# Attention scores: two products of 128 rows each in place of one of 128 and one of 64 rows

## The chip, the cores and the metric

The kernel runs on one core of a Trainium2 chip. The metric is the device time of one execution in microseconds (us), the median of several runs. The engines are written as in the profile: PE is the matrix engine (PEld its weight load, PEq its sequencer), DVE the vector engine, ACT the scalar engine, POOL GpSimd, SP the engine that issues the transfers (SPq is its queue).

## The reference

One layer of a decoder trunk on 256 tokens of width 1024, in float32. Only the two attention branches matter here:

```
h = rms_norm(x, norm_mix_g);  proj = h @ w_in
qa, ka, va, qc, kc, vc, rx, rgate, gates = split(proj)
# branch a: 8 heads of 64; one block of 256 keys, so causal attention with ALiBi
l = einsum('bhqd,bhkd->bhqk', q, k) * 64**-0.5 - slopes * dist     # -inf where dist < 0
ya = softmax(l) @ v
# branch c: 4 heads, two maps of 64 each
p = softmax(same logits);  w = p[map 0] - lam * p[map 1];  yc = rms_norm(w @ v) ...
# branch b: a linear recurrence.  Then gates, output projection, and a gated MLP with a convolution
```

There are 8 score maps in branch a and 8 in branch c, each of 256 queries by 256 keys with a depth of 64.

## The kernel before

**Arithmetic.** Every factor of a product is split into two float32r parts, a high part (the value rounded by ACT) and a low part (the exact rest, by DVE); a product is the sum of hi·hi, hi·lo and lo·hi. `mm3` (lines 110 to 112) issues these three for the projections, with 256 tokens as moving columns.

**Weight stream.** The weights come in 77 chunks of [128, 2048], 1 MB each, in the order of their use. SP loads a chunk into one of three `raw` buffers (line 86). ACT and DVE split each half of a chunk into `whi` and `wlo` (lines 96 and 97), four halves ahead of PE. Chunks 4 and 5 are q of branch a, 6 and 7 its k, 8 and 9 its v (`va`), 10 to 15 q, k and v of branch c, then gates and branch projections. Half n is the first or second half of chunk n // 2.

**Side work.** Attention, convolution and recurrence are side work of the main stream: the table `SL` names the chunk beside which each piece is written, and a scheduler that also places instructions by its own estimate puts them into each engine's order. Each engine, SP's queue included, works through its order from front to back.

**Scores.** q and k of a branch lie as 4 tiles of 128 rows, two heads of 64 in each. `stack_q` and `stack_k` copy them by transfers from SBUF to SBUF (line 395, 64 rows, 256 KB each) into `QS`, which holds q hi in rows 0 to 63 and q lo in rows 64 to 127 of each of 8 maps, and `KS`, which holds k hi twice. `att_scores` computes a map (tile `a0s` to `a7s`, `c00s` to `c31s`) in two halves of 128 queries, j = 0 and 1, into one PSUM bank. For each, line 458 multiplies QS by KS over 128 rows, (q hi + q lo)·k hi, and line 459 adds q hi·k lo over the 64 rows in which that head lies. Both have 256 keys as columns. DVE then adds the ALiBi distances and takes the row minimum (line 464; of j = 0 it reads 128 keys only), and ACT takes the exponential (line 467).

**Buffers.** Large tiles share SBUF by tags: a tile of a tag waits until the readers of the tile before it are done. `q0` holds `qka` (q hi and k lo of branch a) and later `mg`, the sum of the gated branches; `s10` holds `ocs`, the outputs of branch c.

Of the kernel before, what the change touches and what calls it, by code (L numbers as in the profile page):

```python
# [13 lines left out]
P = 128  # L14
S = 256
# [14 lines left out]

# where the side work goes: the first chunk beside which it is done, and over how many it is spread
SL = dict(norm=(4, 2.0), conv=(18, 5.5), moba=(8, 7.0), lag_a=(3, 5), diff=(16, 3.33), lag_c=(2, 4),
          gate=(19, 4.5), rga=(24, 5.0), rgb=(26, 4.0), rgc=32, rgd=(32, 1.5), rgy=(33, 1.5), df=22, sqa=6, ska=7,
          sqc=14, skc=13, lrgw=16, raw_up=20, h2=16, x1t=5)

# the weights in the order of their use, in chunks of [128, 2048]
ORDER = [(_n, _i) for _n, _c in (("rx", 4), ("qa", 2), ("ka", 2), ("va", 2), ("qc", 2), ("kc", 2), ("vc", 2),
# [10 lines left out]

# columns of the packed per-channel parameters
PC = {}  # L50
# [9 lines left out]
def hybrid_trunk(ctx: ExitStack, tc: tile.TileContext, x, wts, par, rgw, lqk, gf, out):  # L60
# [16 lines left out]

# [1 line left out]
    raws, his, los = {}, {}, {}  # L79
# [9 lines left out]
    def split_to(n):  # L89
        """Halves of chunks, up to the n-th, into a float32r part and the exact rest."""  # L90
        while state["split"] < min(n, 2 * NCHUNK):
            i = state["split"]
            raw = raws[i // 2][:, (i % 2) * HC:(i % 2 + 1) * HC]
            his[i] = wsp.tile([P, HC], F32R, name=f"whi{i}", tag="whi")
            los[i] = wsp.tile([P, HC], F32R, name=f"wlo{i}", tag="wlo")
            A.activation(his[i], raw, AF.Copy)  # L96
            V.tensor_tensor(los[i], raw, his[i].bitcast(F32), ALU.subtract)  # L97
            state["split"] += 1
# [14 lines left out]

# [1 line left out]
    # the first norm's gain comes with x, in the 8 columns before it  # L115
    xg_in = big.tile([P, KD * S + KD], F32, name="xg_in", tag="s0")
# [24 lines left out]

# [1 line left out]
    ones = const.tile([P, P], F32, name="ones")  # L143
# [8 lines left out]
    dist = const.tile([P, S], F32, name="dist")  # L152
    # the first q's are scaled by -1/(8 slope), a power of two, head by head
    qsc = const.tile([P, 4], F32, name="qsc")
    for h in range(8):
        G.memset(qsc[64 * (h % 2):64 * (h % 2) + 64, h // 2:h // 2 + 1], -0.125 * 2.0 ** (h + 1))

# [1 line left out]
    xgh = big.tile([P, KD, S], F32R, name="xgh", tag="s1")  # L159
# [15 lines left out]
    def rstd_of(ss_ap, n, scale, name):  # L175
        """1/sqrt(ss*scale + eps), from a table value and one Newton step."""
        m = work.tile([P, n], F32, name=name + "m", tag="nt_m", bufs=1)
        y = work.tile([P, n], F32, name=name + "y", tag="nt_y", bufs=1)
        t = work.tile([P, n], F32, name=name + "t", tag="nt_t", bufs=1)
        r = work.tile([P, n], F32, name=name + "r", tag="rstd", bufs=1)  # L180
        newton(y, m, t, r, ss_ap, scale)
        return r

    def sumsq_bcast(sq, k, src, name, later=False):
        """Adds tiles k, k+1 of src**2 up in sq; the last call sums over the partitions."""
        A.activation(sq[:, k:k + 2, :], src[:, k:k + 2, :], AF.Square)
        if k:
            (G if k < 6 else V).tensor_tensor(sq[:, 0:2, :], sq[:, 0:2, :], sq[:, k:k + 2, :], ALU.add)
        if k == 6 and not later:
            return sumsq_mm(sq, name)  # L190
# [5 lines left out]

# [1 line left out]
    # tiles 0..3, contraction outermost, so that each piece of x and of the weights is used as it lands  # L198
    rx_banks = [mm_bank(f"rxb{b}") for b in range(2)]
# [29 lines left out]
    def T_chunk(i, name, ah, al, evac, nk=KD, kouter=False):  # L229
        """Chunk of 128-wide output tiles; two tiles a bank; evac(bank, first tile)."""  # L230
        nt = HC // (nk * P)
# [37 lines left out]
    def norm_split(hf, hh, hl, src, gain, rstd, k):  # L269
        """Tiles k, k+1 of the normalised rows in two parts."""  # L270
        for j in (k, k + 1):
            V.scalar_tensor_tensor(hf[:, j, :], src[:, j, :], gain[:, j:j + 1], rstd, op0=ALU.mult, op1=ALU.mult)
        s = slice(k, k + 2)
        A.activation(hh[:, s, :], hf[:, s, :], AF.Copy)
        V.tensor_tensor(hl[:, s, :], hf[:, s, :], hh[:, s, :].bitcast(F32), ALU.subtract)
# [8 lines left out]

# [1 line left out]
    sm = const.tile([P, 12, 8], F32, name="sm")  # L286
# [12 lines left out]
    G.tensor_scalar(sm[:, 7], lam_c, -1.0, 0.0, op0=ALU.mult, op1=ALU.max)  # L299
    # sm[8] = softplus(-lambda); the gates are r = (tanh(.)+1)/2  # L300
    G.tensor_scalar(sm[:, 6], sm[:, 6], 2.0, None, op0=ALU.mult)
# [13 lines left out]

# [1 line left out]
    xr = big.tile([P, KD, S], F32, name="xr", tag="s6")  # L317
# [40 lines left out]
    def rg_b(s):  # L358
        """u = 1/(1+t2), refined from (1+exp)/2; a = (1-t2)*u;  -b = sqrt(t2)*(-u)*(2 i x)."""
        V.tensor_scalar(u0[:, s], u0[:, s], 0.5, 0.5, op0=ALU.mult, op1=ALU.add)  # L360
# [13 lines left out]

# [1 line left out]
    # q and k in two float32r parts; QS holds [q hi; q lo] and KS [k hi; k hi] of one map in its 128 rows, so that  # L376
    # one product gives (q hi + q lo) * k hi
    qk = big.tile([P, 8, S], F32R, name="qka", tag="q0")
# [3 lines left out]
    att = {}  # L382
    for n, tq, tk, t1, t2_ in (("a", None, None, "s0", "s9"), ("c", "q6", "q7", "s1", "s2")):
        att[n] = dict(
# [4 lines left out]
            QS=big.tile([P, 8, S], F32R, name="QS" + n, tag=t1),  # L389
            KS=big.tile([P, 8, S], F32R, name="KS" + n, tag=t2_))  # L390

    def stack(dst, row, src):
        """The heads of src's lower and upper rows, in turn, to 64 rows of dst."""
        for o in range(2):
            nc.sync.dma_start(dst[row:row + 64, o::2, :].bitcast(F32), src[64 * o:64 * o + 64, :, :].bitcast(F32))
# [35 lines left out]
    def stack_k(n):  # L431
        stack(att[n]["KS"], 0, att[n]["kh"])
        stack(att[n]["KS"], 64, att[n]["kh"])

    def v_chunks(i, name, dst):
# [15 lines left out]
    def att_scores(n, u, sl, st, name):  # L451
        """Probabilities of one map, unnormalised, with their reciprocal row sums."""
        t, o = u // 2, 64 * (u % 2)
        d = att[n]
        ps = at_bank(name + "s")
        for j in range(2):
            o_ = ps[:, j * S:(j + 1) * S]
            T.matmul(o_, lhsT=d["QS"][:, u, j * P:(j + 1) * P], rhs=d["KS"][:, u, :], start=True, stop=False)
            T.matmul(o_, lhsT=d["qh"][o:o + 64, t, j * P:(j + 1) * P], rhs=d["kl"][o:o + 64, t, :], start=False,
                     stop=True)  # L460
        mn = work.tile([P, 6], F32, name=name + "mn", tag="mn", bufs=8)
# [76 lines left out]
    def rg_y(s):  # L538
        """yb = h * gelu(gate); tr holds -h."""
        if s.start == 0:  # L540
# [7 lines left out]

# [1 line left out]
    sides = {}  # L550
# [16 lines left out]

    # slots are chunk positions: 4 qa, 6 ka, 8 va, 10 qc, 12 kc, 14 vc, 16 g0, 20 ba, 22 g2, 26 bc, 28 rg, 32 g1
    def slot(what, i, n):
# [98 lines left out]

# [1 line left out]
    x1 = big.tile([P, KD, S], F32, name="x1", tag="s6")  # L670
# [16 lines left out]

# [1 line left out]
    h2f = big.tile([P, KD, S], F32, name="h2f", tag="s7")  # L689
# [28 lines left out]

    # the down projection has the tokens in its rows, and so has all that follows
    x1T = big.tile([P, 2, D], F32, name="x1T", tag="s2")  # L720
# [14 lines left out]
    def finish(h, c):  # L735
        """Residual and norm of the columns c*512.. of 128 tokens."""
        o = slice(c * 512, (c + 1) * 512)
# [17 lines left out]
    for name, idx in FFN_ORDER:  # L755
# [13 lines left out]
        else:  # L769
# [4 lines left out]
            if idx == last - 1:  # L774
                # brings the table in before the end; the value is not used
                A.activation(sm[:, 11], acts[last][:, 1, 0, 0:8].bitcast(F32), AF.Abs_reciprocal_sqrt, bias=eps_s,
                             scale=0.0)
                pos += 1
                continue
            # the last two chunks: one half of the tokens after the other  # L780
            for h, c, i, e in ([(h, c, i, e) for h in range(2) for c in range(2) for i in (last - 1, last)
# [86 lines left out]
```

## Time and profile before

| | |
|---|---|
| Time, median of 3 runs | 501.83 us (503.34, 500.37, 501.83) |
| Span of the profiled execution, first to last instruction | 498.7 us |
| What lies between the median and that span | 3.1 us |
| PE busy | 488.2 us, 98% of the span |
| DVE, ACT busy | 383.3 and 306.6 us, 77% and 61% |
| Mean granted clock of PE | 0.986 |
| Moved by transfers | 90.50 MB, 181 GB/s |

The profiled execution has no time of its own beside its span; the median of the runs stands for it. A matmul's duration in the profile contains the way through the array, so that neighbours overlap; what a matmul costs PE is the distance from its start to the next one's start.

### The profile page before, as it was taken

Reading aid. Unit: us, or ns where it says so; the run is one execution under the profiler, and the core shown is the slowest. Engines: PE = TensorE matmul, PEld = TensorE weight load, DVE = VectorE, ACT = ScalarE, POOL = GpSimd, SP = SyncE. Lnnn points to the kernel's source line nnn. Section 1 sums busy time; section 2 is a strip of 40 time slices with the busy share of each in tenths; the row PEclk is TensorE's granted clock in tenths of the full one; section 3 lists DMA queues with packets and bytes.
Section 4 is the critical chain, followed back from the end, with each engine's and each line's share of the span. In section 5 each row is a group of like instructions: output and inputs, shape, how many; then the busy total and the mean of one; then the engine's idle time right before and its main releaser. Section 6 shows DMA issues by size and latency. Waiting matters only on the chain.

```text
span 498.7 us, 8982 instructions
## 1 busy us (share of the span) xinstructions
PE 488.2 (98%) x3580; PEld 460.7 (92%) x3580; DVE 383.3 (77%) x686; ACT 306.6 (61%) x517; POOL 19.5 (4%) x46
## 2 busy tenths in 40 slices
PE   7999999999999999999999999999999999999994
PEld 6999879978889999999999999999999999999983
DVE  4899975645566759998947687999977787787576
ACT  6756645557467889458654465866755555556562
POOL 2630000000000000000000011000000000000000
PEclk9999989999799999999999999999999999999998
DMA  8955973894224242555655564454554555445402
GB/s 256 340 204 184 265 220 156 211 287 178 87 93 160 86 170 86 191 219 182 240 188 176 208 244 170 170 175 177 202 205 170 175 206 213 168 170 175 163 1 85
DMA packets 18217, 90.50 MB, mean 181 GB/s; under 512 B 1792, under 2 KB 6656, under 8 KB 8448
## 3 DMA queue, kind: packets, MB, share of 16 engines
q1 hardware_dynamic: 18176, 89.94, 51.9%
q8 instruction: 28, 0.46, 0.4%
q14 instruction: 13, 0.11, 0.1%
HBM read 84.69 MB, written 1.05 MB: 172 GB/s over the span
## 4 chain that ended last, share of the span: by engine, by line
PE 96%; DMA 1%; ACT 1%; DVE 1%; issue 0%; SPq 0%; DVEq 0%
PE mm L110 24%; PE mm L111 23%; PE mm L112 23%; PE dn L787 4%; PE dn L788 4%; PE dn L789 4%; DMA xg_in<-in_x_dram 1%; PE vc L445 1%; PE va L447 1%; PE vc L447 1%; PE va L446 1%; PE va L445 1%; PE vc L446 1%; PE oa L496 0%; PE rxb L112 0%
## 5 line engine op out<-in xcount | busy, mean ns | idle before, releaser
L96 ACT ACTIVATE whi<-raw 128x1024 fp32r<-128x1024 f32 x150 | 158.4, 1058 | 141.6 <-PE mm L111 93.8
L97 DVE TENSOR_TENSOR wlo<-raw,whi 128x1024 fp32r<-128x1024 f32 x150 | 183.0, 1223 | 60.4 <-ACT whi L96 58.8
L110 PE MATMUL mm<-hh,whi 128*128 128x256 f32 x320 | 93.6, 292 | 0.0
L111 PE MATMUL mm<-hl,whi 128*128 128x256 f32 x320 | 92.5, 289 | 0.0
L112 PE MATMUL mm<-hh,wlo 128*128 128x256 f32 x320 | 92.4, 289 | 0.0
L110 PE MATMUL mm<-x1h,whi 128*128 128x256 f32 x320 | 91.0, 284 | 0.0
L111 PE MATMUL mm<-x1l,whi 128*128 128x256 f32 x320 | 90.5, 283 | 0.0
L112 PE MATMUL mm<-x1h,wlo 128*128 128x256 f32 x320 | 89.8, 281 | 0.0
L110 PEld LDWEIGHTS mm<-hh,whi 128*128 128x128 f32 x320 | 63.3, 198 | 1.0 <-issue 0.2
L111 PEld LDWEIGHTS mm<-hl,whi 128*128 128x128 f32 x320 | 63.4, 198 | 0.2
L112 PEld LDWEIGHTS mm<-hh,wlo 128*128 128x128 f32 x320 | 63.3, 198 | 0.0
L112 PEld LDWEIGHTS mm<-x1h,wlo 128*128 128x128 f32 x320 | 61.2, 191 | 0.0
L111 PEld LDWEIGHTS mm<-x1l,whi 128*128 128x128 f32 x320 | 60.8, 190 | 0.2
L110 PEld LDWEIGHTS mm<-x1h,whi 128*128 128x128 f32 x320 | 60.3, 188 | 0.2
L787 PE MATMUL dn<-whi,act 128*128 128x512 f32 x88 | 34.5, 392 | 0.0
L788 PE MATMUL dn<-wlo,act 128*128 128x512 f32 x88 | 34.4, 391 | 0.0
L789 PE MATMUL dn<-whi,act 128*128 128x512 f32 x88 | 34.4, 391 | 0.0
L110 PE MATMUL mm<-xgh,whi 128*128 128x256 f32 x96 | 27.1, 282 | 0.0
L111 PE MATMUL mm<-xgl,whi 128*128 128x256 f32 x96 | 26.9, 280 | 0.0
L112 PE MATMUL mm<-xgh,wlo 128*128 128x256 f32 x96 | 26.9, 280 | 0.0
L705 ACT ACTIVATE cv<-us,par_s 128x256 f32<-128x256 f32 x40 | 21.6, 587 | 0.0
L789 PEld LDWEIGHTS dn<-whi,act 128*128 128x128 f32 x88 | 16.5, 188 | 3.7 <-DVE act L716 0.2
(476 smaller groups left out, 1021.2 us busy)
## 6 DMA issues: line engine op xcount, KB each, us to landing
raw<-in_wts_dram SPq DMA_DIRECT2D x75, 1024.0 KB, 4.8
raw<-in_wts_dram SPq DMA_DIRECT2D x3, 512.0 KB, 6.9
KSa<-kha SPq DMA_DIRECT2D x4, 256.0 KB, 7.6
rgw<-in_rgw_dram SPq DMA_DIRECT2D x2, 512.0 KB, 4.2
KSc<-khc SPq DMA_DIRECT2D x4, 256.0 KB, 4.5
xt<-in_x_dram SPq DMA_DIRECT2D x1, 1024.0 KB, 7.4
out_dram<-yo SPq DMA_DIRECT2D x4, 256.0 KB, 2.2
xg_in<-in_x_dram SPq DMA_DIRECT2D x3, 256.0 KB, 6.1
```

Source lines behind the costliest of these rows:

```text
L96: A.activation(his[i], raw, AF.Copy)
L97: V.tensor_tensor(los[i], raw, his[i].bitcast(F32), ALU.subtract)
L110: T.matmul(ps, lhsT=wh, rhs=ah, start=start, stop=False, **kw)
L111: T.matmul(ps, lhsT=wh, rhs=al, start=False, stop=False, **kw)
L112: T.matmul(ps, lhsT=wl, rhs=ah, start=False, stop=stop, **kw)
L445: T.matmul(banks[s], lhsT=hs, rhs=wh3[:, kk], start=(k == 0), stop=False)
L446: T.matmul(banks[s], lhsT=hs, rhs=wl3[:, kk], start=False, stop=False)
L447: T.matmul(banks[s], lhsT=ls, rhs=wh3[:, kk], start=False, stop=(k == 7))
L705: A.activation(cv[:, e, :], src[:, o:o + S], AF.Identity, bias=pc("fb", ch), scale=pc("fw", 88 + ch))
L787: T.matmul(ps, lhsT=hi, rhs=hv[i][e][0][:, o], start=(i == 0 and e == 0), stop=False)
L788: T.matmul(ps, lhsT=hi, rhs=hv[i][e][1][:, o], start=False, stop=False)
L789: T.matmul(ps, lhsT=lo, rhs=hv[i][e][0][:, o], start=False, stop=(i == last and e == 1))
```

## The change

A second stacked tile, `KL`, holds k lo twice, as `KS` holds k hi. Each half of a map is then QS by KS and QS by KL, both over 128 rows: (q hi + q lo)·(k hi + k lo), so that q lo·k lo is computed too. The half j = 0 computes only the 128 keys that its queries can see; j = 1 keeps 256. `KL` takes tag `s10` in branch a and `q0` in branch c; PE no longer reads `qh` and `kl`. Four more transfers of 256 KB stand in each `stack_k`.

```diff
-    for n, tq, tk, t1, t2_ in (("a", None, None, "s0", "s9"), ("c", "q6", "q7", "s1", "s2")):
+    for n, tq, tk, t1, t2_, t3 in (("a", None, None, "s0", "s9", "s10"), ("c", "q6", "q7", "s1", "s2", "q0")):
...
-            KS=big.tile([P, 8, S], F32R, name="KS" + n, tag=t2_))
+            KS=big.tile([P, 8, S], F32R, name="KS" + n, tag=t2_),
+            KL=big.tile([P, 8, S], F32R, name="KL" + n, tag=t3))
...
     def stack_k(n):
         stack(att[n]["KS"], 0, att[n]["kh"])
         stack(att[n]["KS"], 64, att[n]["kh"])
+        stack(att[n]["KL"], 0, att[n]["kl"])
+        stack(att[n]["KL"], 64, att[n]["kl"])
...
-        t, o = u // 2, 64 * (u % 2)
         d = att[n]
         ps = at_bank(name + "s")
         for j in range(2):
-            o_ = ps[:, j * S:(j + 1) * S]
-            T.matmul(o_, lhsT=d["QS"][:, u, j * P:(j + 1) * P], rhs=d["KS"][:, u, :], start=True, stop=False)
-            T.matmul(o_, lhsT=d["qh"][o:o + 64, t, j * P:(j + 1) * P], rhs=d["kl"][o:o + 64, t, :], start=False,
-                     stop=True)
+            w = (j + 1) * P
+            o_ = ps[:, j * S:j * S + w]
+            for i, m in enumerate(("KS", "KL")):
+                T.matmul(o_, lhsT=d["QS"][:, u, j * P:(j + 1) * P], rhs=d[m][:, u, 0:w], start=(i == 0), stop=(i == 1))
```

The other lines of the diff take comments away.

On PE, the first scores of branch a follow the last products of `va`. In a row, the number before the name is the line, then the tile written and the tiles read, and the size; `mm_00` is chunk 10, and its `whi` and `wlo` are numbered. Before:

```order
L447 MATMUL va_771<-whi_774,hl 128x512
L458 MATMUL a0s<-KSa,QSa 128x256
L459 MATMUL a0s<-qka 128x256
L458 MATMUL a0s<-KSa,QSa 128x256
L459 MATMUL a0s<-qka 128x256
L110 MATMUL mm_00_890<-hh,whi_790 128x256
L458 MATMUL a1s<-KSa,QSa 128x256
...
L459 MATMUL a2s<-qka 128x256
L111 MATMUL mm_00_890<-hl,whi_790 128x256
```

Now, at the same place (36 more rows of chunk 10 stand where the second "..." is):

```order
L450 MATMUL va_777<-whi_780,hl 128x512
L462 MATMUL a0s<-KSa,QSa 128x128
L110 MATMUL mm_00_896<-hh,whi_796 128x256
...
L462 MATMUL a1s<-KSa,QSa 128x128
L462 MATMUL a2s<-KSa,QSa 128x128
...
L462 MATMUL a0s<-KLa,QSa 128x128
L462 MATMUL a0s<-KSa,QSa 128x256
L462 MATMUL a0s<-KLa,QSa 128x256
L462 MATMUL a2s<-KLa,QSa 128x128
```

Only the first product of a0, a1 and a2 stays near the old place; the rest of a0, a2 and a1 now follow after 39 to 44 of the 48 rows of chunk 10. From a3 on, each map's four products stand together, where they stood before.

On SP's queue, the transfers into KSa stand between the loads of chunk 11 and chunk 12 (`raw` with a number). Before:

```order
L86 DMA raw_806<-in_wts_dram 128x2048
L395 DMA KSa<-kha 64x4x256 x4
L86 DMA raw_884<-in_wts_dram 128x2048
L86 DMA raw_961<-in_wts_dram 128x2048
...
L86 DMA raw_1259<-in_wts_dram 128x2048
L347 DMA rgw_1458<-in_rgw_dram 128x1024
L395 DMA KSc<-khc 64x4x256 x4
L86 DMA raw_1333<-in_wts_dram 128x2048
```

Now (raw_890 is chunk 12, raw_1343 is chunk 18):

```order
L86 DMA raw_812<-in_wts_dram 128x2048
L396 DMA KSa<-kha 64x4x256 x4
L396 DMA KLa<-qka 64x4x256 x4
L86 DMA raw_890<-in_wts_dram 128x2048
...
L86 DMA raw_1269<-in_wts_dram 128x2048
L396 DMA QSc<-qlc 64x4x256 x2
L396 DMA KSc<-khc 64x4x256 x4
L396 DMA KLc<-klc 64x4x256 x4
L86 DMA raw_1343<-in_wts_dram 128x2048
```

The loads of chunk 12 and of chunk 18 are now behind four more transfers each, the second stack of q of branch c moved behind the load of chunk 17, and the first part of `rgw` moved behind chunk 18. On DVE and ACT the same instructions stand in a slightly other order beside chunks 10 to 13 and 17 to 20.

## Rows read from the trace of the kernel before

**Rows 1.** The page, parts 1 and 4: busy time; the chain by engine.

```profile
PE 488.2 (98%) x3580; PEld 460.7 (92%) x3580; DVE 383.3 (77%) x686; ACT 306.6 (61%) x517; POOL 19.5 (4%) x46
...
PE 96%; DMA 1%; ACT 1%; DVE 1%; issue 0%; SPq 0%; DVEq 0%
```

**Rows 2.** Timeline of PE around a4s: start, duration (us), line, out<-in, rows*columns, moving, count.

```profile
85.19 0.49 PE L490 MATMUL a0t<-ident,a0p 128*128 128x128 f32 x3
85.52 0.49 PE L490 MATMUL a1t<-ident,a1p 128*128 128x128 f32 x3
...
86.05 0.38 PE L459 MATMUL a4s<-qka 64*128 64x256 f32 x1
86.36 0.39 PE L458 MATMUL a4s<-KSa,QSa 128*128 128x256 f32 x1
86.68 0.38 PE L459 MATMUL a4s<-qka 64*128 64x256 f32 x1
86.99 0.38 PE L110 MATMUL mm<-hh,whi 128*128 128x256 f32 x1
87.21 0.28 PE L111 MATMUL mm<-hl,whi 128*128 128x256 f32 x1
87.33 0.28 PE L112 MATMUL mm<-hh,wlo 128*128 128x256 f32 x1
```

**Rows 3.** Windows: length, busy (instructions) of PE, PEld, DVE, ACT, POOL, granted clock, DMA share, GB/s.

```profile
66.00:71.00 5.00, 4.47 (x16) 2.44 (x14) 2.48 (x11) 3.68 (x11) 0.00 (x0) 1.00 0.93 339
71.00:76.00 5.00, 5.00 (x30) 5.00 (x30) 4.14 (x16) 1.69 (x7) 0.00 (x0) 0.66 0.41 138
76.00:122.00 46.00, 46.00 (x314) 40.74 (x313) 26.59 (x62) 25.40 (x55) 0.00 (x0) 1.00 0.70 216
...
126.00:134.00 8.00, 8.00 (x37) 7.20 (x37) 4.34 (x19) 2.98 (x11) 0.00 (x0) 0.57 0.33 124
```

**Rows 4.** Timeline of PE: where the granted clock is 0.50, and c00s.

```profile
72.91 0.41 PE L110 MATMUL mm<-hh,whi 128*128 128x256 f32 x1
73.13 0.42 PE L111 MATMUL mm<-hl,whi 128*128 128x256 f32 x1
...
122.29 0.36 PE L458 MATMUL c00s<-KSc,QSc 128*128 128x256 f32 x1
```

**Rows 5.** Timeline of PE: the two passes of one product of full float32.

```profile
115.58 0.27 PE L497 MATMUL oa<-a2pt,va 128*64 128x128 f32 x1
...
115.69 0.27 PE L497 MATMUL oa<-a2pt,va 128*64 128x128 f32 x1
```

**Rows 6.** Instructions of line 458 and transfers of KSa: ns, and us from issue to landing.

```profile
L458 PEldq EVENT_SEMAPHORE  x12: 51/51/4650, 62.1 to 144.6; - x12
...
DMA to landing us min/median/max: 6.4/7.6/9.0
```

**Rows 7.** PE's waits: us in total, times, longest.

```profile
PE a0s L458 <- issue: 0.5, 1, 0.5
```

**Rows 8.** Timeline of SP's queue: the stacks of k of both branches.

```profile
57.20 3.33 SPq L395 DMA_DIRECT2D KSa<-kha  x4
...
101.88 3.37 SPq L395 DMA_DIRECT2D KSc<-khc  x4
```

**Rows 9.** Windows: the stretch in which KSa moves, and one of weight loads alone.

```profile
59.00:64.00 5.00, 5.00 (x24) 4.14 (x23) 5.00 (x11) 1.69 (x3) 0.00 (x0) 1.00 1.07 175
...
67.00:70.00 3.00, 2.96 (x10) 1.67 (x9) 1.02 (x6) 1.92 (x5) 0.00 (x0) 1.00 1.00 404
```

**Rows 10.** Line 410: k lo of branch a is written (start of first and last).

```profile
L410 DVE TENSOR_TENSOR qka<-qkf,kha x2: 681/682/682, 52.1 to 58.0; 128x512 fp32r<-128x512 f32 x2
```

**Rows 11.** The costliest groups: the split of a half, and the gates' products.

```profile
L97 DVE TENSOR_TENSOR wlo<-raw,whi 128x1024 fp32r<-128x1024 f32 x150 | 183.0, 1223 | 60.4 <-ACT whi L96 58.8
L96 ACT ACTIVATE whi<-raw 128x1024 fp32r<-128x1024 f32 x150 | 158.4, 1058 | 141.6 <-PE mm L111 93.8 <-issue 19.5 <-PE dn L789 7.8
...
L110 PE MATMUL rgg<-rgs 128*128 128x256 f32 x16 | 4.9, 303 | 0.0
```

## The prediction

> **What bounds the kernel now.** I read the busy times first. PE is busy for 98% of the span and holds 96% of the chain that ended last [rows 1]; in the stretch of attention it waited once, for 0.5 us [rows 7]. So time comes off this kernel where PE's own spacing shrinks, and only if nothing else then makes PE wait. The spacing is in the timeline of PE. Behind the four products of map a4s, the products of chunk 12 start 0.12 us apart (87.21, 87.33). The score products start 0.31 us apart (86.05, 86.36, 86.68, 86.99), whether of 128 or of 64 rows, and the first full product behind them costs 0.22 (86.99 to 87.21) [rows 2]. All these have 256 columns, so the columns don't explain it. What is particular to the scores is that each product has another number of rows than the one before; I read the spacing as weights that PE cannot load beside a product with another number of rows.
>
> The windows show a second thing. PE's granted clock is 1.00 at 66 to 71, where the first three maps are computed, then a mean of 0.66 at 71 to 76; and 0.57 at 126 to 134, behind the four maps c00s to c11s that begin at 122.3 [rows 3, 4]. The level there is 0.50, and full products start 0.22 us apart (72.91, 73.13) [rows 4]. Before each fall PE issued little: 16 products in the 5 us of 66 to 71 [rows 3].
>
> **The change, part by part.**
>
> *Spacing of the scores.* 16 maps with 4 products each are 64 products. Before they cost 0.31, as full-row products of 256 columns they cost 0.12: 64 × 0.19 = 12.2 us. The maps stand in 10 groups on PE; behind nine of them a full-row product follows, which costs 0.22 before and 0.12 now: 0.9 us. Together 13.1 us. All of it lies on PE, that is on the path.
>
> *The narrow half.* 32 of the 64 products now have 128 columns. No row shows a split float32r product of 128 columns. From below, half of 0.12 would be 0.06, if columns were all that counts: 32 × 0.06 = 1.9 us more gain. The transposes, single passes over 128 columns, start 0.11 apart (85.19 to 85.52 for three) [rows 2]. From above, a product of full float32 with 128 columns takes two passes 0.11 apart (115.58, 115.69) [rows 5], so 0.22 if the narrow product fell to that rate: 32 × 0.10 = 3.2 us less gain. I take 0.12, as the single pass of 128 columns is the nearest row and is no cheaper than that by more than 0.01.
>
> The Trainium skill (TensorE: Matmul & The Clock Gate, section Back-to-back issue gap) gives about 81 ns for a sustained pair of load and product at 128 columns. By that figure the narrow products would bring an estimated 32 × 0.04 = 1.2 us more; the transposes at 0.11 don't bear it out here.
>
> *The clock.* Two falls: 0.34 × 5 us × 2 = 3.4 us at half clock, and 0.43 × 8 us × 2 = 6.9 us [rows 3], 10.3 us together. In that time a full product costs 0.21 to 0.22 in place of 0.12 [rows 2, 4], so 43 to 44% of it is lost: 4.4 us. With scores at 0.12 PE is as dense there as everywhere else, where the clock is 1.00 in this kernel for 46 us on end although single maps stand in it (76 to 122) [rows 3]. I take the 4.4 us as gained; the bounds are 0 and 4.4.
>
> *The transfers of branch a.* Before, PE's sequencer stood at the first score from 62.1 for 4.65 us, to 66.8, for KSa [rows 6], which cost PE the 0.5 us [rows 7]. That wait stays. KSa was issued from 57.2, 0.83 us each, and landed 6.4 to 9.0 us after issue [rows 6, 8]. KLa is issued right behind it, from 60.5 (57.2 + 3.33), since k lo was written by 58.7 (58.0 + 0.68) [rows 10], before SP gets there. KSa moved while the engines carried 175 GB/s in all [rows 9]; 1 MB of such rows takes 5 to 6 us behind KSa, which ends by 66.8, so KLa lands at 70 to 72.5. PE comes to the first product of KLa 41 rows behind 66.8, at 66.8 + 41 × 0.12 = 71.7. The wait is 0 to 1 us; I take 0.3. Behind it four maps come to DVE and ACT within some 2 us; they have until the transposes of a0 and a1, 48 rows or 6 us later. I put 0.3 us for that.
>
> *Chunk 12 behind KLa.* Its load starts after KLa, at 70 to 72.5, and takes 2.6 us for 1 MB at the 404 GB/s that loads alone reach [rows 9]: landed by 75. Then ACT (1.06) and DVE (1.22) split its first half [rows 11], 2.3 us. PE needs that half 121 rows behind 66.8, six of them transposes: 66.8 + 115 × 0.12 + 6 × 0.11 = 81.3 (86.99 before [rows 2]). So there are 4 us to spare: nothing.
>
> *The transfers of branch c.* KLc stands behind KSc, which began at 101.9 [rows 8] and is needed by c00s at 122.3 [rows 4]. Both ends move earlier by about the same, as KSc waits for the last product of k. Four more issues are 3.4 us, the data 5 to 6 us: hidden by the 20 us. Chunk 18 behind them is first used several chunks later still. Nothing.
>
> *Buffers.* KLc takes `q0` from qka, whose readers are now transfers long done; `mg` in `q0` and `ocs` in `s10` are written from products that stand behind the last scores on PE anyway. Nothing. DVE and ACT do the same work in less time: 26.6 and 25.4 us of 46 at 76 to 122 [rows 3], which may shrink to about 39. Nothing.
>
> **Sum.** 13.1 + 4.4 − 0.3 − 0.3 = 16.9 us. The span of 498.7 becomes 481.8. The runs' median is 3.1 us over the profiled span; with these, 485 us.
>
> **The rivals.**
>
> *The narrow products are dear.* They cost 0.22 each, as two passes of full float32 [rows 5]. For it: every split product of the trace has 256 or more columns. Against it: nothing but the single pass of the transposes. Time 485 + 3.2 = 488.2.
>
> *The clock still falls.* If the wait for KLa or the sums of short waits leave PE thin once or twice, 1.5 to 4.4 us stay lost: 486.5 to 489.4. Against it: maps that stand alone gave no fall at 76 to 122 [rows 3], at the old spacing.
>
> *KLa comes late.* If its last part, issued by 63.9, lands 9 us later, at 73, PE waits 1.2 us; if weights get in between, 3 us, and the clock falls as at 71 before: 485 + 3 + 1.5 = 489.5.
>
> *The change does not do what it says.* The 0.31 could belong to short accumulation groups of two products and not to the rows. Then spacing and clock stay: 501.8. Against it: the gates' products (`rgg`) are groups of three and last 303 ns, near the 280 of the long groups; the score products last 380 [rows 2, 11].
>
> *Slower: chunk 12 starves PE.* It waits on SP behind KLa. Each us by which it lands after 79 costs one; the change loses from 79 + 16.9 = 96 on, 35 us after KLa's first issue. KSa took under 10 us.
>
> *Slower too: the 64-row products were free.* If they ran beside the 128-row ones, the change would add 32 products at 0.12, 3.8 us: 505.6. Against it: each 64-row product is followed after 0.31 us like the others [rows 2]. The rule behind this rival is in the Trainium skill (TensorE: Matmul & The Clock Gate, Part 3, Packing small matmuls): small products in distinct row groups run concurrently; here the trace disagrees, as the rows' 0.31 shows.
>
> **How the numbers follow.** My forecast has 0.45; dear narrow products 0.25; a clock that still falls 0.12; KLa late 0.10; no effect 0.05; slower 0.03 (0.02 for chunk 12, 0.01 for the free row groups). The low end is 485 with narrow products at 0.06 and no waits, 485 − 1.9 − 0.6 = 482.5. The high end takes dear narrow products and half of the clock's loss together, 485 + 3.2 + 2.2 = 490.4. That leaves out the no-effect and slower cases and a part of the late one, less than 2 in 10. A difference of 0.5%, 2.5 us, is about what a measurement of this kernel can tell from none; the first four cases are faster by far more: 0.92, 0.05 and 0.03.
>
> **What would show it.** In the timeline, score products of 256 columns 0.12 us apart and no 0.22 behind them; narrow ones at 0.12 (dear: 0.21 or more). The window of c00s to c11s takes 2 us, where it took over 5. The granted clock stays 1.00 from 66 to 150. PE's waits name KLa's transfers or a whi for less than 1 us in all. The prediction is wrong if score products keep 0.31, if PE's sequencer stands at a0s<-KLa for several us, or if the first products of chunk 12 wait for ACT's whi.

## The result, and the profile after

The changed kernel takes **483.62 us** (median of 483.25, 483.98, 483.99 and 483.08), beside 501.1 us for the kernel before (four runs): a ratio of 0.970, 95% interval [0.9664, 0.9735]. Run again (e5_after below), it took 484.25 beside 499.39, 0.973 [0.9692, 0.9768]. Times here and below are medians without disturbed executions. The forecast was 485.0 (482.5 to 490.4).

The profiled execution took 483.25 us, of which 481.1 are its span; before, the span was 498.7. The page of the changed kernel, parts 1 and 4:

```profile
PE 469.9 (98%) x3580; PEld 451.1 (94%) x3580; DVE 382.6 (80%) x686; ACT 305.4 (63%) x517; POOL 19.7 (4%) x46
...
PE 95%; ACT 1%; DMA 1%; DVE 1%; issue 0%; SPq 0%; DVEq 0%
```

PE issues the same 3580 products as before [rows 1] and holds nearly the same share of the chain; its busy time fell by 18.3 us, about as much as the span (17.6). DVE and ACT do the same work in a shorter span. So PE was made shorter, and nothing else took its place.

Where it became shorter is in the timeline of PE. The changed kernel around a3s (with one weight load, PEld), and further down the group c00s to c11s, which stands behind transposes and is followed by a full product (L110):

```profile
73.08 0.22 PE L462 MATMUL a3s<-KSa,QSa 128*128 128x128 f32 x1
73.08 0.19 PEld L462 LDWEIGHTS a3s<-KLa,QSa 128*128 128x128 f32 x1
73.14 0.27 PE L462 MATMUL a3s<-KLa,QSa 128*128 128x128 f32 x1
73.25 0.33 PE L462 MATMUL a3s<-KSa,QSa 128*128 128x256 f32 x1
73.42 0.28 PE L462 MATMUL a3s<-KLa,QSa 128*128 128x256 f32 x1
73.54 0.28 PE L110 MATMUL mm<-hh,whi 128*128 128x256 f32 x1
73.66 0.28 PE L111 MATMUL mm<-hl,whi 128*128 128x256 f32 x1
...
113.42 0.31 PE L462 MATMUL c00s<-KSc,QSc 128*128 128x128 f32 x1
...
113.97 0.22 PE L462 MATMUL c01s<-KSc,QSc 128*128 128x128 f32 x1
...
115.35 0.28 PE L110 MATMUL mm<-hh,whi 128*128 128x256 f32 x1
```

The four score products take 0.46 us (73.08 to 73.54), and the full product behind them is again 0.12 before the next one. Before, the steps of a4s were 0.29 (from 85.76) and three times 0.31, and then 0.22 for the full product [rows 2]. The four narrow and wide products are not evenly spaced: 0.06, 0.11, 0.17, 0.12. The first narrow one is cheap, and the first wide one behind the narrow ones gives it back.

Windows of the changed kernel (columns as in [rows 3]):

```profile
66.00:71.00 5.00, 5.00 (x44) 5.00 (x43) 3.06 (x6) 1.62 (x3) 0.00 (x0) 1.00 1.09 293
71.00:76.00 5.00, 5.00 (x45) 5.00 (x44) 3.66 (x22) 3.51 (x15) 0.00 (x0) 1.00 0.98 403
76.00:122.00 46.00, 46.00 (x347) 42.76 (x346) 32.46 (x88) 32.13 (x75) 0.00 (x0) 1.00 0.87 248
126.00:134.00 8.00, 8.00 (x70) 8.00 (x70) 5.68 (x21) 6.55 (x19) 0.00 (x0) 1.00 0.47 169
```

At 66 to 71 PE issues 44 products where it issued 16, and the granted clock stays at 1.00, where it was 0.66 at 71 to 76 and 0.57 at 126 to 134 [rows 3].

All of PE's waits of the changed kernel, and what answers to [rows 6, 8]: the sequencer's waits at line 462, the landing of KSa; the issue of KLa's four parts (ns, first and last start) and their landing.

```profile
PE rxb L110 <- ACT whi L209: 2.1, 3, 1.0
PE warm L147 <- DVE eps_s L149: 1.0, 1, 1.0
PE rxb L112 <- DVE wlo L210: 0.8, 2, 0.7
```

```profile
L462 PEldq EVENT_SEMAPHORE  x10: 51/51/2273, 61.9 to 112.1; - x10
```

```profile
DMA to landing us min/median/max: 5.1/5.6/5.9
```

```profile
L396 SPq DMA_DIRECT2D KLa<-qka x4: 688/786/1010, 60.4 to 63.1; - x4
...
DMA to landing us min/median/max: 5.9/6.3/6.9
```

PE waits at the start of the kernel only, for `rxb` and `warm`, and for neither stack in the stretch of attention of this execution. The sequencer stood for KSa until 61.9 + 2.27 = 64.2, before 66.8. KLa's last part was issued at 63.1 and landed within 6.9 us, by 70.0; its first reader, a0s, starts at 70.97.

The starts of some tiles on PE, from the timelines of both kernels:

| | before | after | earlier by | gain to the next row |
|---|---|---|---|---|
| a0s | 66.84 | 65.96 | 0.88 | 4.22 (a0, a1, a2, first fall of the clock) |
| a3s | 78.18 | 73.08 | 5.10 | 0.79 (one map) |
| a4s | 85.76 | 79.87 | 5.89 | 0.79 (one map) |
| a5s | 93.09 | 86.41 | 6.68 | 2.19 (a5, a6, a7) |
| c00s | 122.29 | 113.42 | 8.87 | 6.05 (c00 to c11, second fall) |
| c20s | 137.21 | 122.29 | 14.92 | 1.57 (two maps) |
| c30s | 146.12 | 129.63 | 16.49 | 1.59 (two maps) |
| first `oc` | 162.93 | 144.85 | 18.08 | |

Nine maps lie where the clock was full before: 0.79 + 0.79 + 2.19 + 1.57 + 1.59 = 6.93 us, 0.77 a map, 12.3 us for 16. The other seven maps bring 4.22 + 6.05 = 10.27, that is 4.9 us more than 7 × 0.77: the clock, as a remainder. The 0.88 at a0s is mostly the 0.5 that PE waited there before [rows 7]. At the end 17.65 of the 18.08 are left.

### The profile page after: what moved, and what is told of

Same layout as the page of the kernel before. It is cut to its first block, busy times and chain, and to the rows that moved or that the text cites. A ratio compares the mean times of both kernels' runs of the same rounds, so it can differ in the third digit from the quotient of the medians.

```text
span 481.1 us, 8975 instructions
## 1 busy us (share of the span) xinstructions
PE 469.9 (98%) x3580; PEld 451.1 (94%) x3580; DVE 382.6 (80%) x686; ACT 305.4 (63%) x517; POOL 19.7 (4%) x46
## 4 chain that ended last, share of the span: by engine, by line
PE 95%; ACT 1%; DMA 1%; DVE 1%; issue 0%; SPq 0%; DVEq 0%
PE mm L110 24%; PE mm L111 24%; PE mm L112 24%; PE dn L789 4%; PE dn L790 4%; PE dn L791 4%; DMA raw<-in_wts_dram 1%; PE va L450 1%; PE vc L448 1%; PE va L448 1%; PE va L449 1%; PE vc L450 1%; PE vc L449 1%; PE oa L498 0%; PE rxb L112 0%; PE rgg L110 0%
## 5 line engine op out<-in xcount | busy, mean ns | idle before, releaser
L110 PE MATMUL mm<-x1h,whi 128*128 128x256 f32 x320 | 90.9, 284 | 0.0
L110 PE MATMUL mm<-hh,whi 128*128 128x256 f32 x320 | 90.9, 284 | 0.0
L112 PE MATMUL mm<-hh,wlo 128*128 128x256 f32 x320 | 90.5, 283 | 0.0
L111 PE MATMUL mm<-hl,whi 128*128 128x256 f32 x320 | 90.5, 283 | 0.0
L110 PEld LDWEIGHTS mm<-hh,whi 128*128 128x128 f32 x320 | 61.3, 192 | 0.1
L111 PEld LDWEIGHTS mm<-hl,whi 128*128 128x128 f32 x320 | 61.3, 192 | 0.0
L112 PEld LDWEIGHTS mm<-hh,wlo 128*128 128x128 f32 x320 | 61.3, 192 | 0.0
L110 PEld LDWEIGHTS mm<-x1h,whi 128*128 128x128 f32 x320 | 60.2, 188 | 0.2
L110 PE MATMUL mm<-xgh,whi 128*128 128x256 f32 x96 | 27.0, 282 | 0.0
L717 ACT ACTIVATE act<-cv 128x256 fp32r<-128x256 f32 x22 | 9.1, 412 | 17.4 <-DVE cv L713 17.4
```

Source lines behind the costliest of these rows:

```text
L110: T.matmul(ps, lhsT=wh, rhs=ah, start=start, stop=False, **kw)
L111: T.matmul(ps, lhsT=wh, rhs=al, start=False, stop=False, **kw)
L112: T.matmul(ps, lhsT=wl, rhs=ah, start=False, stop=stop, **kw)
```

## The experiments

Two explanations stand against each other in most of these. The theory: a product costs about 0.12 us whether it has 128 or 256 columns, a change of the number of rows between two products costs extra, and the slow stretches let the clock fall. The rivals are named with each. Where an expectation gives a time, it counts from the 501.1 us of the kernel before; beside the experiments that kernel took 498.53 us (e1 to e4) and 499.39 us (e5 to e8), so the gains are what can be compared.

**e2_grouped: fewer changes of the row count.** In the kernel before, each map's products are put in the order 128, 128, 64, 64 rows, with the same stacks, products and sums. One more thing differs: the two accumulation groups of two products become one of four (`start` and `stop`).

```diff
-            T.matmul(o_, lhsT=d["QS"][:, u, j * P:(j + 1) * P], rhs=d["KS"][:, u, :], start=True, stop=False)
-            T.matmul(o_, lhsT=d["qh"][o:o + 64, t, j * P:(j + 1) * P], rhs=d["kl"][o:o + 64, t, :], start=False,
-                     stop=True)
+            T.matmul(ps[:, j * S:(j + 1) * S], lhsT=d["QS"][:, u, j * P:(j + 1) * P], rhs=d["KS"][:, u, :],
+                     start=(j == 0), stop=False, skip_group_check=True)
+        for j in range(2):
+            T.matmul(ps[:, j * S:(j + 1) * S], lhsT=d["qh"][o:o + 64, t, j * P:(j + 1) * P],
+                     rhs=d["kl"][o:o + 64, t, :], start=False, stop=(j == 1), skip_group_check=True)
```

> The kernel before, with the same four products of a map in another order: both of 128 rows, then both of 64. Theory: a product costs 0.31 where the number of rows changes and 0.12 where it stays, so two changes per map instead of four: spacing 0.12, 0.31, 0.12, 0.31, a gain of 32 x 0.19 = 6.1 us, 495.0, and 490.6 if the clock then doesn't fall. Rival, short groups: all stay at 0.31, 501.1. Rival, products of 64 rows are slow in themselves: only the second of 128 rows gains, 16 x 0.19 = 3.0 us, 498.1.

Measured: 489.39 us beside 498.53, ratio 0.982 [0.976, 0.989], a gain of 9.1 where 6.1 was expected and 10.5 if the clock doesn't fall. The timeline of PE around a3s of this kernel:

```profile
74.61 0.39 PE L457 MATMUL a3s<-KSa,QSa 128*128 128x256 f32 x2
74.93 0.50 PE L460 MATMUL a3s<-qka 64*128 64x256 f32 x2
75.36 0.38 PE L110 MATMUL mm<-hh,whi 128*128 128x256 f32 x1
75.58 0.28 PE L111 MATMUL mm<-hl,whi 128*128 128x256 f32 x1
```

The same map in the kernel before, with some of its weight loads (PEld):

```profile
78.06 0.19 PEld L458 LDWEIGHTS a3s<-KSa,QSa 128*128 128x128 f32 x1
78.18 0.28 PE L458 MATMUL a3s<-KSa,QSa 128*128 128x256 f32 x1
...
78.39 0.18 PEld L459 LDWEIGHTS a3s<-qka 64*128 64x128 f32 x1
78.39 0.38 PE L459 MATMUL a3s<-qka 64*128 64x256 f32 x1
...
78.70 0.39 PE L458 MATMUL a3s<-KSa,QSa 128*128 128x256 f32 x1
...
79.02 0.38 PE L459 MATMUL a3s<-qka 64*128 64x256 f32 x1
...
79.33 0.39 PE L110 MATMUL mm<-hh,whi 128*128 128x256 f32 x1
...
79.55 0.28 PE L111 MATMUL mm<-hl,whi 128*128 128x256 f32 x1
```

In e2, the two products of 128 rows and the step to 64 rows take 0.32 (74.61 to 74.93), the two of 64 rows and the step back 0.43, the next one 0.22. From 74.61 to 75.58 are 0.97 us for five products, 0.60 at 0.12: two changes of the row count cost 0.37, **0.19 each**. Before, the same five took 1.37 (78.18 to 79.55: 0.21, three times 0.31, 0.22) with four changes, 0.77 too much, 0.19 each. That a product of 64 rows is dear in itself is thereby out: there are as many as before. The sum of two products as the cause is not out by e2 alone, which has sums of four; it is out by the changed kernel, whose sums have two products each and take 0.46 for four (a3s above), and by e6 below, where they have 256 columns and start 0.12 apart.

The weight loads show where the price comes from. Between products of equal rows a load starts ahead of its own product, beside the one before it: at 78.06 for the product at 78.18, and in the changed kernel at 73.08 for the product at 73.14. The load of the 64-row product starts at 78.39, together with its product; in e2 the loads at both changes do the same (74.93 and 75.36). So here a load did not start beside a product with another number of rows, as the forecast had read it from the spacing alone. The Trainium skill (TensorEngine Tiling (Array Packing), section Key Properties) says that a change of tiling mode drains TensorE, without a figure; these rows agree and give it the price. The granted clock did not fall in this execution: it is 1.00 in every window from 66 to 130.

**e3_all64 and e8_all64: no change of the row count within a map, but all products of 64 rows.** Each half is q hi·k hi, q lo·k hi and q hi·k lo, 96 products in all; the stacks and their transfers are gone.

```diff
-            T.matmul(o_, lhsT=d["QS"][:, u, j * P:(j + 1) * P], rhs=d["KS"][:, u, :], start=True, stop=False)
-            T.matmul(o_, lhsT=d["qh"][o:o + 64, t, j * P:(j + 1) * P], rhs=d["kl"][o:o + 64, t, :], start=False,
-                     stop=True)
+            for i, (x, y) in enumerate((("qh", "kh"), ("ql", "kh"), ("qh", "kl"))):
+                T.matmul(o_, lhsT=d[x][o:o + 64, t, j * P:(j + 1) * P], rhs=d[y][o:o + 64, t, :], start=(i == 0),
+                         stop=(i == 2))
```

> The kernel before with three products of 64 rows per half map, hi by hi, lo by hi and hi by lo, from the tiles as they are, and no stacks: 96 products in place of 64, no transfers from SBUF to SBUF. Theory: 0.12 between them, as their rows don't change, and 0.2 more at both ends of a group: 96 x 0.12 + 10 x 0.4 = 15.5 us where the scores of before took 20.8, so 5 us gained, and 4.4 if the clock doesn't fall: 491.5 to 496. Rival, products of 64 rows are slow in themselves: 96 x 0.31 = 29.8 us, 510. Rival, products in the two row halves run beside each other: below 490.

> All scores as 96 products of 64 rows, once more, for an undisturbed profile. The times of this kernel were 488.4 to 489.3. Theory A: products of 64 rows in opposite halves of the array run beside each other where neighbours on PE lie in opposite halves, so some start 0.01 to 0.06 apart, and a map on its own has 0.12 within it and 0.2 at its ends: six products in 0.8 to 0.9 us. Theory B: no product runs beside another; all stand at 0.12 or more, and the time under 490 comes from the clock alone, which does not fall.

Measured: e3 488.73 us beside 498.53, ratio 0.980 [0.975, 0.985], a gain of 9.8 where 5 was expected, and 9.4 if the clock doesn't fall; e8 488.26 us in its one execution, whose rows are shown. The timeline of PE around a0s to a3s of e8:

```profile
66.20 0.28 PE L457 MATMUL a0s<-qka 64*128 64x256 f32 x1
66.21 0.38 PE L457 MATMUL a1s<-kha,qka 64*128 64x256 f32 x1
66.32 0.28 PE L457 MATMUL a0s<-kha,qka 64*128 64x256 f32 x1
...
73.20 0.28 PE L112 MATMUL mm<-hh,wlo 128*128 128x256 f32 x1
73.41 0.38 PE L457 MATMUL a3s<-kha,qka 64*128 64x256 f32 x1
73.64 0.28 PE L457 MATMUL a3s<-kha,qla 64*128 64x256 f32 x1
73.75 0.28 PE L457 MATMUL a3s<-qka 64*128 64x256 f32 x1
...
74.11 0.27 PE L457 MATMUL a3s<-qka 64*128 64x256 f32 x1
74.31 0.39 PE L110 MATMUL mm<-hh,whi 128*128 128x256 f32 x1
74.53 0.28 PE L111 MATMUL mm<-hl,whi 128*128 128x256 f32 x1
```

Two things are seen. Map a3s stands alone: its inner products are 0.12 apart, and only the way in (0.21 and 0.23) and out (0.20 and 0.22) are longer. Its six products take 0.90. And a0 and a1 lie in opposite halves of the array's rows; where they are neighbours, two products start 0.01 apart (66.20 and 66.21), and the pair takes about the time of one (0.12 to 66.32). So the concurrency that the forecast's last rival spoke of exists, between 64-row products of opposite halves. In the kernel before, each 64-row product stands between products of 128 rows, and the starts of neighbours there are 0.21 us apart or more. Theory A of e8 holds. What the pairs are worth in time, beside a clock that does not fall, no run separates. The kernel is 5.1 us of span behind the changed one (486.2 and 481.1); a map that stands alone takes 0.90 in place of 0.46.

**e1_wide and e6_wide: the narrow half, taken away.** The changed kernel with 256 columns in both halves; e6 is e1 once more, with more runs and beside the changed kernel itself (e5_after).

```diff
-            w = (j + 1) * P
+            w = S
```

> The changed kernel with 256 columns in both halves of a map (nothing else differs). Theory: a product costs PE the load of its weights as well, and 128 columns save next to nothing: a map takes 0.48 us of PE in place of 0.46, 16 maps 0.3 us, so 483.9. Rival: the narrow half is a part of the gain, 32 products at half the cost: 32 x 0.06 = 1.9 us slower, 485.5.

> The changed kernel itself, beside the next two on one chip, as the base for them. Every theory: 483 to 484.5 us, with PE's granted clock at 1.00 throughout.

> The changed kernel with 256 columns in both halves of a map (the first half computes 128 keys more, which nobody reads). Theory: a product costs PE about 0.12 us whether it has 128 or 256 columns, so the 32 wider products cost 32 x 0.01 = 0.3 us more than the changed kernel on the same chip, 483.9. Rival: the narrow products run at half the price, 0.06 each, and are worth 32 x 0.06 = 1.9 us: 485.5 us.

Measured: e1 484.38 us, 0.8 above the 483.62 of the changed kernel, which did not run beside it; e6 485.12 us, 0.9 above e5's 484.25 on the same chip. That lies between 0.3 and 1.9, and the runs of e5 and e6 reach over 3.5 and 4.5 us (483.98 to 487.43, 483.01 to 487.49), so the times decide nothing. The profiled execution of e6 lost time in places that have nothing to do with the width: 1.4 us of waits for KSa, and a clock below 1.00 ahead of the first score. The timeline tells it. The group c00s to c11s of e6, four maps behind transposes as in the changed kernel above:

```profile
117.53 0.36 PE L462 MATMUL c00s<-KSc,QSc 128*128 128x256 f32 x1
...
118.09 0.28 PE L462 MATMUL c01s<-KSc,QSc 128*128 128x256 f32 x1
118.21 0.28 PE L462 MATMUL c01s<-KLc,QSc 128*128 128x256 f32 x1
118.33 0.28 PE L462 MATMUL c01s<-KSc,QSc 128*128 128x256 f32 x1
...
119.52 0.28 PE L110 MATMUL mm<-hh,whi 128*128 128x256 f32 x1
```

The group takes 1.99 us here (117.53 to 119.52) and 1.93 with the narrow half (113.42 to 115.35). Eight narrow products are thus worth 0.06 us, and the narrow half 0.2 to 0.3 us in all, as the theory said.

**e4_spread: the clock at the scores of branch c.** The kernel before, with two numbers of `SL` changed, so that c10 and c11 start some 7 us behind the end of c01 and no longer right behind it; the later pairs and what follows them move too. The products and their spacing are those of before.

```diff
-SL = dict(norm=(4, 2.0), conv=(18, 5.5), moba=(8, 7.0), lag_a=(3, 5), diff=(16, 3.33), lag_c=(2, 4),
-          gate=(19, 4.5), rga=(24, 5.0), rgb=(26, 4.0), rgc=32, rgd=(32, 1.5), rgy=(33, 1.5), df=22, sqa=6, ska=7,
+SL = dict(norm=(4, 2.0), conv=(18, 5.5), moba=(8, 7.0), lag_a=(3, 5), diff=(16, 4.0), lag_c=(2, 4),
+          gate=(19, 4.5), rga=(24, 5.0), rgb=(26, 4.0), rgc=32, rgd=(32, 1.5), rgy=(33, 1.5), df=23, sqa=6, ska=7,
```

> The kernel before with the four pairs of branch c beside chunks 16, 17, 18 and 19, where two pairs stood beside 16; the 64 products are the same. Theory: the second fall of the clock comes from 16 products in a row at 0.31; eight in a row bring none: 6.9 us at half clock are gone, 3 us gained, 498. Rival: the fall belongs to something else at that place, or to the number of score products: it stays, 501.

Measured: 495.96 us (10 runs) beside 498.53 (13 runs), ratio 0.9955 [0.9925, 0.9985]: 2.6 us less. Windows of e4:

```profile
66.00:71.00 5.00, 5.00 (x19) 3.23 (x18) 3.22 (x17) 4.10 (x14) 0.00 (x0) 0.85 0.65 267
71.00:76.00 5.00, 5.00 (x37) 5.00 (x37) 3.92 (x12) 1.57 (x4) 0.00 (x0) 0.81 0.54 193
...
126.00:134.00 8.00, 8.00 (x57) 6.54 (x56) 5.23 (x16) 4.87 (x12) 0.00 (x0) 1.00 0.51 159
```

The second fall is gone in this execution: 57 products at 126 to 134, 37 before [rows 3]. The first one stayed. At half clock for 6.9 us, with 43% lost, the second fall was counted at 3.0 us; 2.6 measured agrees, though its interval, 0.7 to 3.7 us, is wide.

**e7_extra: the added transfers alone.** The kernel before, in which KL is filled in both branches at the place of SP's queue that it has in the changed kernel, and nobody reads it. In branch c it lies in `s10`, not in `q0`.

```diff
+            KL=big.tile([P, 8, S], F32R, name="KL" + n, tag=t3))
...
+        stack(att[n]["KL"], 0, att[n]["kl"])
+        stack(att[n]["KL"], 64, att[n]["kl"])
```

> The kernel before with the added transfers alone: KL is filled in both branches as in the changed kernel, at the same place of the queue, and nobody reads it; the scores are those of before. (KL of both branches lies in s10.) Theory: the transfers are hidden, so the time is that of the kernel before, within 0.5 us of it (with its own spread between runs). Rival: the loads of chunks 12 and 18 behind them come late, PE waits for a whi beside branch a or c, and the time is 1 to 4 us over that of before.

Measured: 499.13 us beside 499.39, ratio 1.000 [0.997, 1.003]. PE has no wait in it beyond the three of the start. The added 2 MB cost nothing that 1.4 us of uncertainty would show.

## Why the prediction was right, and where it was not

**The spacing** (13.1 us forecast): 12.3 by the starts of the nine maps at full clock. The mechanism, a price on each change of the row count, is shown by e2 together with the changed kernel, e6 and the weight loads. e2 and the changed kernel, both without a fall of the clock in the profiled execution, differ by 487.2 − 481.1 = 6.1 us of span: what the two remaining changes a map cost, 16 × 0.37 = 5.9. The term was 0.8 too large because it took one step for every place. It read 0.31 as the price of every score product from a4s, which stands behind transposes; the first product of a3s, behind a full product, cost 0.21 (78.18 to 78.39). It took 0.12 for every score product afterwards; a map right behind transposes takes 0.55 (113.42 to 113.97) and not 0.46. And the last product of a7s, which a product with 64 of the array's columns follows (`oa`, 106.24), still costs 0.21 in the changed kernel (from 106.03); whether through the columns or the type, no run separates.

**The narrow half** (taken at 0.12, bounds 0.06 and 0.22): right, 0.11 to 0.12 on average by the timeline. Neither the 0.22 of the dear rival nor the 0.06 of the low bound occurred over a map. The nearest row, a single pass of 128 columns at 0.11, was the right one to choose.

**The clock** (4.4 forecast): 4.9 by the starts, which includes what else changed at those two places; 2.6 (0.7 to 3.7) of it measured by e4 for the second fall. The clock stayed at 1.00 through the attention of the changed kernel. The rival in which it still falls did not come true.

The executions of the kernel before that ran beside the experiments, 30 in all, price the clock without any change of the program. The two with the highest mean granted clock, 0.998, have spans of 493.2 and 493.5 us; the 13 with 0.986 or less, as in the profiled one, have 497.3 to 499.7, in the middle 497.9. That is 4.5 us for the falls, near the forecast. Without them the kernel before is still 11.5 us above the changed one (in the middle 481.9 in its five executions at 0.997 or 0.998), close to the 12.3 of the spacing. The forecast took both falls from one trace as certain, and many executions of the kernel before have only a part of them: that may be why the gain is 17.5 us in one comparison and 15.1 in the other.

**The transfers of branch a.** "That wait stays" was wrong. The 0.5 us at a0s did not come back. In both kernels the stack of k has the same place on SP's queue; the sequencer stood for it until 64.2 and not 66.8, and until 64.2 to 65.9 in e2, e4, e5 and e7, two of which have the queue of before. In e6, whose queue is that of the changed kernel, it came last of all (the last row is of e5):

```profile
L462 PEldq EVENT_SEMAPHORE  x16: 51/51/4951, 64.1 to 132.3; - x16
...
PE a0s L462 <- issue: 0.8, 1, 0.8
PE a1s L462 <- DMA KSa<-kha: 0.6, 1, 0.6
...
PE c11s L462 <- ACT a6pt L494: 1.1, 1, 1.1
```

There PE waits 1.4 us, and the sequencer stands until 69.0 (64.1 + 4.95). About 2 us of that are a later issue (59.1 in place of 57.0); the rest is the way from issue to landing, at most 9.1 us in e6 and at most 5.9 in the changed kernel's first trace. A forecast from one trace should have given this wait a range and not a value. KLa was forecast to land at 70 to 72.5 and to cost 0.3; it landed by 70.0 and cost nothing. In e6 its last part, issued at 65.4, was 9.1 to 10.2 us on the way, to 74.5 at the earliest, and its first reader started at 75.36: the rival in which KLa comes late was near. The 0.3 for DVE and ACT was not spent in the first trace of the changed kernel; in e5, the same kernel, PE stands 1.1 us at c11s for ACT (last row above). The forecast put nothing on DVE and ACT at that place.

**Chunk 12, the transfers of branch c, the buffers** (nothing each): right in the traces taken. The first product of chunk 12 starts at 80.41, 81.3 forecast, without a wait; e7 shows the transfers to be hidden; that `q0` holds nobody up is seen in the changed kernel only, which names no wait for it.

**The sum.** The span fell by 17.6 (16.9 forecast): spacing 12.3, clock 4.9, the wait at a0s and the start 0.9; at the end 0.4 is lost again. That it comes so near the forecast is in part luck: the spacing brought 0.8 less, but the start and the waits came out 1.5 better (0.9 at a0s, and the 0.6 set aside for waits). Of the 1.4 us by which 485.0 missed, half is the span. The other half is the way the sum was closed: 3.1 us were added to the span as what lies between it and the median. In every execution here with both times known the step is 1.9 to 2.2 us (483.25 and 481.1, 489.36 and 487.2, 488.26 and 486.2, for example). By that the profiled execution of before took 500.6 to 500.9 us and was 1 us quicker than the median taken for it.

**The slower rivals.** Chunk 12 did not starve. The free 64-row products: the mechanism is real (e8), but the row on which the forecast dismissed it, each 64-row product followed after 0.31, holds for the order of before only.

## What to carry to other kernels

Where PE is the bound, look for products whose neighbour uses another number of rows: each change cost 0.19 us here, more than a whole product at 0.12, so that more arithmetic in full rows, or the same products grouped by their rows, is faster. Halving the columns of a product from 256 to 128 brought next to nothing here, 0.06 us for eight products, since a product of 128 columns cost nearly the same 0.12. And a stretch of thin issue is paid twice if the clock falls behind it, so look at the granted clock of the windows behind each such stretch, and in more than one execution before you count it as a gain.

## What was not expected of the hardware

The price of a change of rows is split over two products: 0.20 to 0.21 for the last one of the old kind and 0.22 to 0.23 for the first of the new, in place of 0.12 each (e8: 73.20, 73.41, 73.64 and 74.11, 74.31, 74.53). 64-row products in opposite halves of the rows start 0.01 us apart when they are neighbours.

The falls of the clock come and go between executions of one kernel: the mean granted clock of the 30 executions above goes from 0.982 to 0.998. In the trace of e7, whose scores are those of before, the window 71 to 76 has 1.00 (0.66 before), while the second fall is there:

```profile
71.00:76.00 5.00, 5.00 (x42) 4.81 (x40) 3.06 (x11) 0.49 (x3) 0.00 (x0) 1.00 0.98 389
...
122.00:126.00 4.00, 4.00 (x11) 2.47 (x12) 3.02 (x15) 2.71 (x13) 0.00 (x0) 0.67 0.46 193
126.00:134.00 8.00, 8.00 (x54) 7.74 (x54) 5.37 (x15) 4.19 (x12) 0.00 (x0) 0.74 0.35 117
```

With it goes the spread of the times of the kernel before, 495.4 to 501.7 us in the 17 runs beside e7. In e6 PE issued only 20 products at 66 to 71, as it waited for KSa, and the clock stayed at 1.00 behind it. Which thin stretch makes it fall, and which doesn't, stays open.
